# A two-layer encoder trunk on one core: layer 0's u and v projections as three float32r passes instead of one exact float32 pass

## The chip, the cores and the metric

The kernel runs on one core of a Trainium2 chip. The metric is the device time of one execution in microseconds. Times inside the profile count from the start of the profiled span.

## The reference

Two layers, 256 tokens, width 2048. Each layer modulates a layer-normed input by a vector computed from `c`, projects it once into the columns of four head groups, mixes, projects back, and runs a gated convolutional FFN. Cut to what matters here:

```python
for l in range(DEPTH):
    mod = (silu(c) @ w_mod[l] + b_mod[l]).reshape(bn, 6, d)
    shift_m, scale_m, gate_m = mod[:, 0, None], mod[:, 1, None], mod[:, 2, None]
    ...
    h = layer_norm(x) * (1.0 + scale_m) + shift_m
    proj = h @ w_in[l]                       # 2048 -> 4288 columns
    uv, q_c, kv_c, k_r, sb, sc, sh, ag = jnp.split(proj, IN_SPLITS, axis=-1)
    y_a = gmlp_mixer(uv, ...)                # u * (W_s LN(gelu(v)) + b), 512 columns each
    y_b, y_c, y_d = mla_mixer(...), short_conv_mixer(sb, sc, sh, ...), conformer_conv(ag, ...)
    y = jnp.concatenate([y_a, y_b, y_c, y_d], axis=-1) @ w_out[l]
    x = layer_norm(ALPHA * x + (1.0 + gate_m) * y, ...)
    ...                                      # FFN, residual, layer norm
```

## The kernel before

A matmul has two forms. The exact one takes float32 operands. The other takes float32r operands: a tile is split into `hi` (a cast on ScalarE) and `lo` (the difference, on VectorE), and the product is three matmuls, hi·hi, hi·lo and lo·hi. Nearly all of the kernel uses the second form; layer 0's input projection and a few other pieces use the first.

Layer 0's input projection starts in `by_blocks`. The contraction dimension of 2048 is cut into 16 blocks `kt` of 128. The modulation is not known yet, so its shift and scale for one block are computed just ahead of it, and all products that can be started with that block follow:

- two 1 MB tiles `wmod` are loaded and reduced on VectorE (L193, one instruction of 128x2048 each); a small add (`mod`, L1485) finishes the block's two columns, and ScalarE applies them in place to the normed, transposed input (`hF<-hF,mod`, L120, 128x256). `hF` of a block is ready after that;
- D: 1024 columns, 8 products of 128x256 into `accD`; U: 512 columns, 4 of 128x256 into `accU`; V: 512 columns with tokens as rows, 2 of 128x512 into `accV`. Their weights are two tiles `wexact` of 512 KB;
- after each batch of four blocks come E's products for the four (512 columns, two more tiles). `accV` and `accE` share two PSUM buffers, so each is copied away by ScalarE (`partV`, `partE`) at the end of its batch, and the copies of the batches are added on VectorE (L1324).

After `by_blocks` come the latent group B, group C, the attention steps and the output projection; then the FFN and layer 1. In the trace one exact product is two MATMUL records.

The order on each engine is set at build time by a scheduler that places instructions by readiness and program order; at run time each engine takes them in that order. All loads stand on SP's queue. Buffers: 4 for `wmod`, 4 of each of two tags for weight tiles (`wexact` takes the tags in turn), 11 tiles of 4 KB a partition in the pool `slot`, of which `hF` holds four, and 10 in the pool `act`. A load waits on the queue until its buffer is released.

Of the kernel before, what the change touches and what calls it, by code (L numbers as in the profile page):

```python
# [7 lines left out]
F32 = mybir.dt.float32  # L8
F32R = mybir.dt.float32r
AF = mybir.ActivationFunctionType  # L10
ALU = mybir.AluOpType
AX = mybir.AxisListType

P = 128
D = 2048
S = 256
DEPTH = 2
W_G = 512
KT = D // P
# [6 lines left out]
C_UV, C_Q, C_SB, C_SC, C_AG = 0, 1024, 1728, 2240, 3264  # L26
# [21 lines left out]

BATCHES = ((0, 4), (4, 4), (8, 4), (12, 4))

FEED_US, BLOCK_US, LEAD_US = 2.7, 0.432, 6.0

UQ_ORDER = [h * 192 + c for h in range(4) for c in range(128)] + [h * 192 + 128 + c for h in range(4) for c in range(64)]

# [26 lines left out]
def rows_of(l, k0, nk, c0, width):  # L81

    return lambda a: a[l, k0 * P : (k0 + nk) * P, c0 : c0 + width].reshape(nk, P, width).transpose(1, 0, 2)
# [3 lines left out]
def encoder_kernel(ctx: ExitStack, tc: tile.TileContext, A: dict, consts: bass.AP, out: bass.AP):  # L87
    nc = tc.nc
    pe, act, dve, pool = nc.tensor, nc.scalar, nc.vector, nc.gpsimd
# [3 lines left out]
    splitp = ctx.enter_context(tc.tile_pool(name="splitp", bufs=4))  # L93
# [16 lines left out]
    def ms_tile(name):  # L110
        return msp.tile([P, 512], F32, tag="ms", name=name)

    def acc_tile(name):
        return accp.tile([P, 512], F32, tag="acc", name=name)

    def mm(o, lhsT, rhs, start, stop):
        pe.matmul(o, lhsT, rhs, start=start, stop=stop, skip_group_check=True)  # L117
# [4 lines left out]
    def slot(name, dtype=F32):  # L122
        return slotp.tile([P, 1024], dtype, tag="slot", name=name)
# [41 lines left out]
    at = [16 + l * 425 for l in range(DEPTH)]  # L165
# [10 lines left out]
    def rest_of_constants():  # L176
        nc.sync.dma_start(out=par[:, 112:PARAMS], in_=A["params"][:, 112:PARAMS])
        nc.sync.dma_start(out=cst[:, 128:1024], in_=consts[:, 128:1024])
        plus_one(0, SCALE_F, GATE_M, GATE_F)
        plus_one(1, SCALE_M, SCALE_F, GATE_M, GATE_F)  # L180
# [131 lines left out]
    exact_turn = [0]  # L312
# [38 lines left out]
    def act_pair(name):  # L351

        both = actp.tile([P, 4 * S], F32R, tag="act", name=name).rearrange("p (k h t) -> p k h t", k=2, h=2)
        return [both[:, :, 0, :], both[:, :, 1, :], both]
# [6 lines left out]
    def split(dst, src):  # L361
        hi, lo = dst[:2]
        act.copy(hi, src)  # L363
        dve.tensor_tensor(out=lo, in0=src, in1=hi.bitcast(F32), op=ALU.subtract)  # L364
# [907 lines left out]
    def by_blocks(l, w_in, hF, first_mod, quarter, mix_d, mix_u, gelu_v, mix_v, mix_b, mix_c, mix_e):  # L1272


        hf = lambda kt: hF[kt // 4][:, kt % 4, :]
        accD = [acc_tile(f"D{l}_c{i}") for i in range(4)]
        accU = [acc_tile(f"U{l}_c{i}") for i in range(2)]
        parts = {"V": [], "E": []}

        blocks = [lambda kt=kt, m=m: first_mod(kt, m) for kt in range(KT) for m in (SHIFT_M, SCALE_M)]  # L1280
        at = {"mods": 0, "dma": 10.0, "dve": 15.0, "pe": 0.0}
        ready = {}

        def mods_for(kt):

            while at["mods"] < len(blocks) and (
                at["mods"] < 2 * (kt + 1) or at["pe"] - at["dma"] > LEAD_US
            ):
                modulated = blocks[at["mods"]]()
                at["dma"] += FEED_US  # L1290
                at["dve"] = max(at["dve"], at["dma"] + 1.6) + 2.4
                ready[at["mods"] // 2] = at["dve"] + 1.0
                at["mods"] += 1
                if at["mods"] in (2, 4, 6):
                    quarter(at["mods"] // 2, modulated)
                if at["mods"] == 8:
                    rest_of_constants()

        def load(kt, nk, c0, width):

            mods_for(kt + nk - 1)
            got = weights(w_in, kt, nk, c0, width, True)
            at["dma"] += FEED_US * nk * width / 2048
            at["pe"] = max(at["pe"], at["dma"] + 1.6, ready[kt + nk - 1]) + nk * width / P * BLOCK_US
            return [w for w, _ in got]

        def channels(ps, kt, w, start, stop):
            for i in range(w.shape[1] // P):
                o = ps[i // 2][:, (i % 2) * S : (i % 2 + 1) * S]
                mm(o, w[:, i * P : (i + 1) * P], hf(kt), start and i % 2 == 0, stop)  # L1310

        def keep_part(g, ps):
            if len(parts[g]) < len(BATCHES) - 1:
                both = actp.tile([P, 1024], F32, tag="act", name=f"part{g}")
                for i in range(2):
                    act.copy(both[:, i * 512 : (i + 1) * 512], ps[i])
                parts[g].append(both)
            else:
                parts[g].append(ps)

        def total(g):
            *sums, ps = parts[g]
            for other in sums[1:]:
                dve.tensor_tensor(out=sums[0], in0=sums[0], in1=other, op=ALU.add)  # L1324
            halves = [sums[0][:, i * 512 : (i + 1) * 512] for i in range(2)]
            for i in range(2):
                dve.tensor_tensor(out=halves[i], in0=ps[i], in1=halves[i], op=ALU.add)
            return halves

        quarter(0, None)  # L1330
        mods_for(0)
        for k0, nkt in BATCHES:
            accV = [ms_tile(f"V{l}_{t}") for t in range(2)]
            for kt in range(k0, k0 + nkt):
                d, uv = load(kt, 1, C_AG, 1024)[0], load(kt, 1, C_UV, 1024)[0]

                def product_v(kt=kt, uv=uv):
                    for t in range(2):
                        mm(accV[t], hf(kt)[:, t * P : (t + 1) * P], uv[:, 512:], kt == k0, kt == k0 + nkt - 1)

                def product_du(kt=kt, d=d, uv=uv):
                    channels(accD, kt, d, kt == 0, kt == KT - 1)
                    channels(accU, kt, uv[:, :512], kt == 0, kt == KT - 1)

                for product in (product_v, product_du) if kt == k0 + nkt - 1 else (product_du, product_v):
                    product()
            keep_part("V", accV)
            if k0 + nkt == KT:
                mix_d(accD, None)
                mix_u(accU, None)  # L1350
                for t, v in enumerate(total("V")):
                    gelu_v(t, v)
            es = []
            for kt in range(k0, k0 + nkt, 2):
                es.extend(load(kt, 2, C_SB, 512))
            accE = [ms_tile(f"E{l}_{i}") for i in range(2)]
            for kt, w in enumerate(es, k0):
                channels(accE, kt, w, kt == k0, kt == k0 + nkt - 1)
            keep_part("E", accE)
        sumE = total("E")  # L1360
        postponed.append(mix_v)
        phase(l, "B")
        run(latent_group(w_in, C_Q, f"B{l}", mix_b, hF=hf, bg=STEPS[l]["B"]))
        phase(l, "C")

        def mix_ce(cps, tps):
            mix_c(cps, tps)
            mix_e(sumE, None)

        run(group(w_in, C_SC, 1024, f"C{l}", mix_ce, hF=hf, bg=STEPS[l]["C"]), 2)  # L1370
# [154 lines left out]
    for l in range(DEPTH):  # L1525
        Y = {}
        if l == 0:
            hF = [slot(f"hF{q}").rearrange("p (j s) -> p j s", j=4) for q in range(4)]
            quarter, powers = normed_T(hF)
            mixers(l, (A["w_in"], l), Y, hF, first_mod_of(hF, powers), quarter)  # L1530
        else:
            mixers(l, (A["w_in"], l), Y)
        phase(l, "out")
        out_proj(
            l,
            "out",
            (A["w_out"], l),
            lambda i, Y=Y: Y["abcd"[i]],
            list(range(KT)),
            gate(l, GATE_M),  # L1540
            f"o{l}",
            A["post_mix_g"][l],
            A["post_mix_b"][l],
            needs(l, SHIFT_F, SCALE_F),
            modulated(l, SHIFT_F, SCALE_F),
            plain=(1024, 1536) if l == 0 else (),
            bg=STEPS[l]["out"],
        )
        phase(l, "up")
        G = []  # L1550
        ffn_up(l, G)
        phase(l, "down")
        out_proj(
            l,
            "down",
            (A["ffn_w_down"], l),
            lambda i, G=G: G[i],
            list(range(NF)),
            gate(l, GATE_F),
            f"d{l}",  # L1560
            A["post_ffn_g"][l],
            A["post_ffn_b"][l],
            needs(l + 1, SHIFT_M, SCALE_M) if l + 1 < DEPTH else None,
            modulated(l + 1, SHIFT_M, SCALE_M) if l + 1 < DEPTH else None,
        )
# [88 lines left out]
```

## Time and profile before

| | us |
|---|---|
| median of 3 runs | 2214.95 (2213.76 to 2219.54) |
| profiled execution | 2214.94 |
| its span | 2213.2 |
| `by_blocks` on TensorE: first product to the first of B | 21.03 to 161.73 |
| one block of D, U and V inside a batch | 6.90 |
| one batch (E end to E end) | 34.49 |

The profiled execution is the median run to 0.01 us; 1.74 us lie outside its span. Over the whole span TensorE (PE) is busy 99%, VectorE (DVE) 77%, ScalarE (ACT) 49%. Busy of PE is modelled from the records of matmuls and hides gaps of a fraction of a microsecond, so the pace of PE is read from the starts of its rows. A row of the timeline gives start, duration, engine, line, operation, output and inputs, shape and count, and in brackets the idle time just before it and what ended it.

### The profile page before, as it was taken

The numbers are of one execution on the slowest core, as the hardware profiler recorded it, in microseconds if no ns is written. First come the engines' busy times: TensorE is split into PE (matmuls) and PEld (weight loads), VectorE is DVE, ScalarE is ACT, GpSimd is POOL, SyncE is SP. The second block draws the span as 40 slices with busy tenths as digits, with TensorE's granted clock in tenths as the row PEclk, the third lists the DMA queues.
The fourth block names the chain that finished last, engine by engine and source line by source line (L and its number), as shares of the span: only waits on it lengthen the run. The fifth ranks groups of instructions, "written<-read, shape, count | busy, mean of one in ns | idle before, by whom it ended". The sixth has DMA issues, their size and how long they took to land. (4 is left out here: it accounts for less than half of the span.)

```text
span 2213.2 us, 28318 instructions
## 1 busy us (share of the span) xinstructions
PE 2185.3 (99%) x10852; PEld 1794.0 (81%) x10852; DVE 1702.1 (77%) x2265; ACT 1075.7 (49%) x1652; POOL 22.4 (1%) x38
## 2 busy tenths in 40 slices
PE   9999999999999999999999999999999999999997
PEld 6776875588888888888867988868888888888886
DVE  5657996799898888989958988877765656565776
ACT  3132730655454545545665455465444545464553
POOL 0000000000000000000000000000000000000000
PEclk9999999999999999999999999999999999999999
DMA  9999889598888888888757547856765555555553
GB/s 391 417 376 391 358 332 390 210 350 324 310 333 318 327 313 324 344 332 326 285 215 294 189 157 255 316 210 246 265 211 190 190 190 191 190 210 192 191 195 145
DMA packets 94730, 608.15 MB, mean 275 GB/s; under 512 B 10689, under 2 KB 10881, under 8 KB 29313
## 3 DMA queue, kind: packets, MB, share of 16 engines
q1 hardware_dynamic: 94466, 606.31, 74.0%
q8 instruction: 85, 1.39, 0.2%
q14 instruction: 51, 0.42, 0.0%
q10 hardware_dynamic: 128, 0.03, 0.0%
HBM read 604.17 MB, written 2.13 MB: 274 GB/s over the span
## 5 line engine op out<-in xcount | busy, mean ns | idle before, releaser
L345 DVE TENSOR_TENSOR wlo<-wraw,whi 128x1024 fp32r<-128x1024 f32 (+1 forms) x608 | 729.0, 1214 | 286.3 <-ACT whi L344 273.1
L344 ACT CAST whi<-wraw 128x1024 fp32r<-128x1024 f32 (+1 forms) x608 | 630.9, 1045 | 635.4 <-PE g_c L117 207.8
L193 DVE SCALAR_TENSOR_TENSOR wmod<-wmod,crep 128x2048 f32<-128x2048 f32 x192 | 438.4, 2287 | 72.0 <-DMA wmod<-in_w_mod_dram 71.1
L117 PE MATMUL v_c<-hT,whi 128*128 128x512 f32 x1408 | 489.7, 393 | 0.0
L117 PE MATMUL g_c<-hT,whi 128*128 128x512 f32 x1280 | 445.0, 392 | 0.0
L117 PE MATMUL v_c<-hT,wlo 128*128 128x256 f32 x1408 | 392.5, 279 | 0.0
L117 PE MATMUL d<-whi,a 128*128 128x512 f32 x1344 | 386.5, 389 | 0.0
L117 PE MATMUL g_c<-hT,wlo 128*128 128x256 f32 x1280 | 356.8, 279 | 0.4 <-DVE wlo L345 0.4
L117 PEld LDWEIGHTS v_c<-hT,whi 128*128 128x128 f32 x1408 | 263.6, 187 | 59.2
L117 PEld LDWEIGHTS d<-whi,a 128*128 128x128 f32 x1344 | 252.0, 188 | 52.4
L117 PEld LDWEIGHTS g_c<-hT,whi 128*128 128x128 f32 x1280 | 239.7, 187 | 54.1
L117 PEld LDWEIGHTS v_c<-hT,wlo 128*128 128x128 f32 x1408 | 265.4, 188 | 0.2
L117 PEld LDWEIGHTS g_c<-hT,wlo 128*128 128x128 f32 x1280 | 241.2, 188 | 0.7 <-DVE wlo L345 0.7
L117 PE MATMUL d<-wlo,a 128*128 128x512 f32 x672 | 232.9, 389 | 0.0
L117 PEld LDWEIGHTS d<-wlo,a 128*128 128x128 f32 x672 | 126.1, 188 | 26.2
L363 ACT CAST a<-g 128x512 fp32r<-128x512 f32 x132 | 81.3, 617 | 63.8 <-PE d L117 63.2
L364 DVE TENSOR_TENSOR a<-g,a 128x512 fp32r<-128x512 f32 x132 | 89.0, 686 | 5.1 <-ACT a L363 5.1
L117 PE MATMUL o<-whi,a 128*128 128x512 f32 x320 | 91.6, 393 | 0.0
L501 PE MATMUL first<-wexact,hN 128*128 128x512 f32 x192 | 85.5, 595 | 1.4 <-ACT hN L120 1.0
L1415 DVE SCALAR_TENSOR_TENSOR u<-g,par,u 128x254 f32<-128x254 f32 (+1 forms) x176 | 73.8, 477 | 0.0
L117 PEld LDWEIGHTS o<-whi,a 128*128 128x128 f32 x320 | 60.6, 190 | 12.7
L501 PEld LDWEIGHTS first<-wexact,hN 128*128 128x128 f32 x192 | 35.3, 190 | 41.2 <-issue 34.9
(311 smaller groups left out, 2174.0 us busy)
## 6 DMA issues: line engine op xcount, KB each, us to landing
wmod<-in_w_mod_dram SPq DMA_DIRECT2D x192, 1024.0 KB, 7.2
wraw<-in_ffn_w_up_dram SPq DMA_DIRECT2D x168, 1024.0 KB, 5.1
wraw<-in_ffn_w_down_dram SPq DMA_DIRECT2D x88, 1024.0 KB, 5.0
wexact<-in_w_in_dram SPq DMA_DIRECT2D x64, 512.0 KB, 11.0
wraw<-in_w_in_dram SPq DMA_DIRECT2D x24, 1024.0 KB, 6.1
wraw<-in_w_out_dram SPq DMA_DIRECT2D x22, 1024.0 KB, 6.0
wexact<-in_w_out_dram SPq DMA_DIRECT2D x20, 512.0 KB, 11.6
wexact<-in_ffn_w_up_dram SPq DMA_DIRECT2D x16, 512.0 KB, 5.7
```

The lines of the kernel that those rows point to most:

```text
L117: pe.matmul(o, lhsT, rhs, start=start, stop=stop, skip_group_check=True)
L193: i = dve.scalar_tensor_tensor(out=raw, in0=raw, scalar=1.0, in1=crep, op0=ALU.mult, op1=ALU.mult, accum_out=col)
L344: held(act.copy(hi[:, :m], r), "cast")
L345: i = dve.tensor_tensor(out=lo[:, :m], in0=r, in1=hi[:, :m].bitcast(F32), op=ALU.subtract)
L363: act.copy(hi, src)
L364: dve.tensor_tensor(out=lo, in0=src, in1=hi.bitcast(F32), op=ALU.subtract)
L501: i = pe.matmul(ps, hN[kt // 4][:, kt % 4, t * P : (t + 1) * P], parts[kt], start=kt == 0, stop=kt == KT - 1, skip_group_check=True,)
L1415: dve.scalar_tensor_tensor(out=u[:, sh:], in0=x[:, : S - sh], scalar=col(k, j), in1=u[:, sh:], op0=ALU.mult, op1=ALU.add)
```

## The change

For every block, the 1024 columns of u and v are loaded into one tile `wuv` (same size and buffers as before) and split: ScalarE casts 128x1024 into `hi_uv`, VectorE subtracts into `lo_uv`, both in tiles of the pool `slot`. The block's `hF` is split too: ScalarE casts 128x256 into the first half of `h`, VectorE subtracts into the second. V becomes 6 products of 128x512 and U 12 of 128x256 in float32r. D and E stay exact. Each block's loads now stand as two `wmod`, D's tile, `wuv`; before, one `wexact` stood between the two `wmod` at most blocks. Three tiny memsets on GpSimd touch `hF`'s later tiles at the start, so that they hold their slots.

```diff
+        def load_split(kt):
+            at["dma"] += FEED_US / 2
+            at["pe"] = max(at["pe"], at["dma"] + 3.0, ready[kt]) + 8 * SPLIT_US
...
+            raw = splitp.tile([P, 1024], F32, tag=tag, name="wuv")
...
+            hi, lo = slot("hi_uv", F32R), slot("lo_uv", F32R)
+            act.copy(hi, raw)
+            dve.tensor_tensor(out=lo, in0=raw, in1=hi.bitcast(F32), op=ALU.subtract)
+            if kt % 2 == 0:
+                halves["h"] = act_pair("h")
+            h = [x[:, kt % 2, :] for x in halves["h"][:2]]
+            split(h, hf(kt))
+            return hi, lo, h
...
-                d, uv = load(kt, 1, C_AG, 1024)[0], load(kt, 1, C_UV, 1024)[0]
...
+                d = load(kt, 1, C_AG, 1024)[0]
+                hi, lo, (xh, xl) = load_split(kt)
+                st, sp = kt == k0, kt == k0 + nkt - 1
+                if not sp:
+                    channels(accD, kt, d, kt == 0, False)
+                for t in range(2):
+                    tok = slice(t * P, (t + 1) * P)
+                    mm(accV[t], xh[:, tok], hi[:, 512:], st, False)
+                    mm(accV[t], xh[:, tok], lo[:, 512:], False, False)
+                    mm(accV[t], xl[:, tok], hi[:, 512:], False, sp)
+                if sp:
+                    channels(accD, kt, d, False, kt == KT - 1)
+                st, sp = kt == 0, kt == KT - 1
+                for i in range(4):
...
+                    mm(o, hi[:, off], xh, st and i % 2 == 0, False)
+                    mm(o, hi[:, off], xl, False, False)
+                    mm(o, lo[:, off], xh, False, sp)
...
+            for q in range(1, 4):
+                pool.memset(hF[q][:, 0, 0:1], 0.0)
```

The new instructions take places in the order of VectorE and ScalarE. VectorE from the second half of block 9 to the modulation of block 10 (`sums_9` is block 9's pair of `wmod`, the x2 is both of block 10's, `partE` the addition of the batches' E). Before:

```order
L193 SCALAR_TENSOR_TENSOR wmod,sums_9_544<-wmod,crep 128x2048
L1324 TENSOR_TENSOR partE<-partE 128x1024
L193 SCALAR_TENSOR_TENSOR wmod,sums_9_544<-wmod,crep 128x2048
L1485 TENSOR_TENSOR mod_9_553<-sums_9_544,par 128x2
L193 SCALAR_TENSOR_TENSOR wmod,sums_10_572<-wmod,crep 128x2048 x2
L1485 TENSOR_TENSOR mod_10_581<-sums_10_572,par 128x2
```

VectorE in the same stretch after the change:

```order
L193 SCALAR_TENSOR_TENSOR wmod,sums_9_695<-wmod,crep 128x2048
L364 TENSOR_TENSOR h<-hF_120,h 128x256
L1344 TENSOR_TENSOR partE<-partE 128x1024
L1320 TENSOR_TENSOR lo_uv<-wuv,hi_uv 128x1024
L193 SCALAR_TENSOR_TENSOR wmod,sums_9_695<-wmod,crep 128x2048
L1512 TENSOR_TENSOR mod_9_739<-sums_9_695,par 128x2
L364 TENSOR_TENSOR h<-hF_120,h 128x256
L1320 TENSOR_TENSOR lo_uv<-wuv,hi_uv 128x1024
L193 SCALAR_TENSOR_TENSOR wmod,sums_10_778<-wmod,crep 128x2048 x2
L1512 TENSOR_TENSOR mod_10_785<-sums_10_778,par 128x2
```

Both subtractions of block 9 now stand ahead of block 10's two reductions, and those of block 8 ahead of the second reduction of block 9. ScalarE in the same stretch, from block 8's modulation to block 10's, before:

```order
L120 ACTIVATE hF_120<-hF_120,mod_8_514 128x256
L1316 COPY partE<-E_0_521 128x512
L1316 COPY partE<-E_1_522 128x512
L120 ACTIVATE hF_120<-hF_120,mod_9_553 128x256
L120 ACTIVATE hF_120<-hF_120,mod_10_581 128x256
```

ScalarE there after the change:

```order
L120 ACTIVATE hF_120<-hF_120,mod_8_667 128x256
L1336 COPY partE<-E_0_672 128x512
L363 CAST h<-hF_120 128x256
L1336 COPY partE<-E_1_673 128x512
L1319 CAST hi_uv<-wuv 128x1024
L120 ACTIVATE hF_120<-hF_120,mod_9_739 128x256
L363 CAST h<-hF_120 128x256
L1319 CAST hi_uv<-wuv 128x1024
L120 ACTIVATE hF_120<-hF_120,mod_10_785 128x256
```

Each block's cast of the weights stands behind that block's own modulation and its cast of `hF`. In the first batch the order is a little different; VectorE there from block 0's sum to block 2's reductions, before:

```order
L1485 TENSOR_TENSOR mod_0_198<-sums_0_191,par 128x2
L193 SCALAR_TENSOR_TENSOR wmod,sums_1_221<-wmod,crep 128x2048 x2
L1485 TENSOR_TENSOR mod_1_244<-sums_1_221,par 128x2
L193 SCALAR_TENSOR_TENSOR wmod,sums_2_265<-wmod,crep 128x2048 x2
```

VectorE in that stretch after the change:

```order
L1512 TENSOR_TENSOR mod_0_201<-sums_0_194,par 128x2
L1320 TENSOR_TENSOR lo_uv<-wuv,hi_uv 128x1024
L193 SCALAR_TENSOR_TENSOR wmod,sums_1_259<-wmod,crep 128x2048
L364 TENSOR_TENSOR h<-hF_118,h 128x256
L193 SCALAR_TENSOR_TENSOR wmod,sums_1_259<-wmod,crep 128x2048
L1512 TENSOR_TENSOR mod_1_266<-sums_1_259,par 128x2
L1320 TENSOR_TENSOR lo_uv<-wuv,hi_uv 128x1024
L364 TENSOR_TENSOR h<-hF_118,h 128x256
L193 SCALAR_TENSOR_TENSOR wmod,sums_2_321<-wmod,crep 128x2048 x2
```

Here too each block's subtractions stand ahead of the next block's reductions; on ScalarE two normalising `xn` stand between a block's modulation and its cast of the weights in blocks 0 to 2. Behind `by_blocks` the four compute engines' order is that of before but for a few neighbours that change places on VectorE in group B.

More of the change, by code (lines that the diff above doesn't have):

```diff
@@ L49 @@
 BATCHES = ((0, 4), (4, 4), (8, 4), (12, 4))
-FEED_US, BLOCK_US, LEAD_US = 2.7, 0.432, 6.0
+FEED_US, BLOCK_US, SPLIT_US, LEAD_US = 2.7, 0.432, 0.35, 6.0
 UQ_ORDER = [h * 192 + c for h in range(4) for c in range(128)] + [h * 192 + 128 + c for h in range(4) for c in range(64)]
@@ L1305, in load @@
             return [w for w, _ in got]
+        halves = {}
+        def load_split(kt):
+            at["dma"] += FEED_US / 2
+            at["pe"] = max(at["pe"], at["dma"] + 3.0, ready[kt]) + 8 * SPLIT_US
+            tag = ("whi", "wlo")[exact_turn[0] % 2]
+            exact_turn[0] += 1
+            raw = splitp.tile([P, 1024], F32, tag=tag, name="wuv")
+            w, l = w_in
+            nc.sync.dma_start(out=raw, in_=w.take(1024, rows_of(l, kt, 1, C_UV, 1024)))
+            hi, lo = slot("hi_uv", F32R), slot("lo_uv", F32R)
[6 more added lines that the diff above has]
+            return hi, lo, h
         def channels(ps, kt, w, start, stop):
@@ L1334, in by_blocks @@
             for kt in range(k0, k0 + nkt):
-                d, uv = load(kt, 1, C_AG, 1024)[0], load(kt, 1, C_UV, 1024)[0]
[L1337 to L1346, printed above, removed]
+                d = load(kt, 1, C_AG, 1024)[0]
[12 more added lines that the diff above has]
+                for i in range(4):
+                    o = accU[i // 2][:, (i % 2) * S : (i % 2 + 1) * S]
+                    off = slice(i * P, (i + 1) * P)
+                    mm(o, hi[:, off], xh, st and i % 2 == 0, False)
+                    mm(o, hi[:, off], xl, False, False)
+                    mm(o, lo[:, off], xh, False, sp)
             keep_part("V", accV)
```

## The prediction

> **What bounds the kernel now.** I read the page's first lines for the whole, then the stretches of the changed stage, then each engine's timeline there.
>
> ```profile
> PE 2185.3 (99%) x10852; PEld 1794.0 (81%) x10852; DVE 1702.1 (77%) x2265; ACT 1075.7 (49%) x1652; POOL 22.4 (1%) x38
> 92.75:127.24 34.49, 34.49 (x145) 27.36 (x144) 21.04 (x22) 4.74 (x8) 0.00 (x0) 1.00 1.02 417
> 162.00:201.00 39.00, 39.00 (x143) 25.69 (x142) 33.64 (x36) 9.58 (x27) 0.00 (x0) 1.00 0.93 367
> ```
>
> The first row says that TensorE (PE) never rests for long, so what lengthens or shortens its chain shows in the end. The second is the third batch of `by_blocks` (after the time: PE, weight loads, VectorE, ScalarE, GpSimd, granted clock, DMA share, GB/s): PE full, VectorE busy 21 of 34 us, ScalarE 5, the DMA engines full at 417 GB/s. The third is group B, full on PE. Inside the batch PE goes from block to block without a stop:
>
> ```profile
> 92.75 3.62 PE L117 MATMUL D_c<-hF,wexact 128*128 128x256 f32 x16
> 96.20 1.89 PE L117 MATMUL U_c<-hF,wexact 128*128 128x256 f32 x8
> 97.93 1.88 PE L117 MATMUL V<-wexact,hF 128*128 128x512 f32 x4
> 99.64 3.62 PE L117 MATMUL D_c<-hF,wexact 128*128 128x256 f32 x16
> 120.33 7.07 PE L117 MATMUL E<-hF,wexact 128*128 128x256 f32 x32
> 127.24 3.62 PE L117 MATMUL D_c<-hF,wexact 128*128 128x256 f32 x16
> 161.73 0.81 PE L117 MATMUL B_w<-wexact,hF 128*128 128x384 f32 x2
> ```
>
> From start to start D takes 3.45 us, U 1.73, V 1.71, a block 6.9, E 6.91. The stage ends at 161.73, where B starts.
>
> **The change: PE's own work.** A float32r product's pace stands in layer 1:
>
> ```profile
> 1205.68 2.08 PE L117 MATMUL Da_c<-hT,wlo 128*128 128x256 f32 x16
> 1207.59 3.82 PE L117 MATMUL Da_c<-hT,whi 128*128 128x512 f32 x16
> 1211.25 2.08 PE L117 MATMUL Da_c<-hT,wlo 128*128 128x256 f32 x16
> ```
>
> 16 of 128x256 take 1.91 us, 0.119 each; 16 of 128x512 take 3.66, 0.229 each. So V becomes 6 x 0.229 = 1.37 us, U 12 x 0.119 = 1.43. A block goes from 6.9 to 6.25 us, and 16 blocks save 16 x 0.64 = 10.2 us of PE work. That is the whole gain, if PE remains the one that ends last.
>
> **What must be ready for a block.** The added conversions are small beside the idle time of their engines, but they stand in strict order with what makes the next block's input:
>
> ```profile
> 131.61 2.28 DVE L193 SCALAR_TENSOR_TENSOR wmod<-wmod,crep 128x2048 f32<-128x2048 f32 x1
> 133.82 2.28 DVE L193 SCALAR_TENSOR_TENSOR wmod<-wmod,crep 128x2048 f32<-128x2048 f32 x1
> 136.15 0.16 DVE L1485 TENSOR_TENSOR mod<-sums,par 128x2 f32<-128x2 f32 x1
> 136.34 0.60 ACT L120 ACTIVATE hF<-hF,mod 128x256 f32<-128x256 f32 x1 [4.02 <-DVE mod L1485]
> L344 ACT CAST whi<-wraw 128x1024 fp32r<-128x1024 f32 x592 | 618.3, 1052 | 615.0 <-PE g_c L117 207.8 <-PE v_c L117 153.2 <-PE d L117 136.0
> L345 DVE TENSOR_TENSOR wlo<-wraw,whi 128x1024 fp32r<-128x1024 f32 x592 | 714.7, 1222 | 286.3 <-ACT whi L344 273.1 <-issue 5.5 <-PE Da_c L117 2.0
> L363 ACT CAST hT<-hN 128x512 fp32r<-128x512 f32 x24 | 14.5, 617 | 0.0
> 153.30 0.60 ACT L785 ACTIVATE sg<-D_c 128x512 f32<-128x512 f32 x1 [0.27 <-PE D_c L117]
> 153.93 0.69 DVE L786 TENSOR_TENSOR gluD<-D_c,sg 128x512 f32<-128x512 f32 x1 [0.17 <-ACT sg L785]
> ```
>
> Reductions follow each other by 2.21 us, the sum comes 2.33 after the second, `hF` starts 0.19 later and takes 0.60. Casts of 512 and 1024 columns take 0.617 and 1.052, so one of 256 about 0.40. The subtraction of 1024 takes 1.22, and I let the next instruction start 1.15 after it. ScalarE hands to VectorE in 0.03 (153.30 + 0.60 to 153.93).
>
> After the change VectorE may start block k+1's reductions only behind block k's `lo_uv`, which waits for block k's cast of the weights, which on ScalarE stands behind block k's `hF` and its cast. The loop from `hF` to the next `hF` is therefore 0.60 + 0.03 (cast of `hF` starts) + 0.40 + 1.05 + 0.03 + 1.15 + 2.21 + 2.33 + 0.19 = 7.99 us. The small subtraction (about 0.4) lies beside the cast of the weights. Against 6.25 on PE, PE now waits about 1.7 us ahead of each such block, and its saving is gone inside the batch.
>
> **Batches 2 to 4.** Does E's time let VectorE run ahead? No: the cast of the next batch's first block stands behind the first copy of E, and its weights' cast behind the second.
>
> ```profile
> 92.08 0.59 ACT L1316 COPY partE<-E 128x512 f32<-128x512 f32 x1 [2.82 <-PE E L117]
> 92.95 0.59 ACT L1316 COPY partE<-E 128x512 f32<-128x512 f32 x1 [0.28 <-PE E L117]
> 93.56 1.23 DVE L1324 TENSOR_TENSOR partE<-partE 128x1024 f32<-128x1024 f32 x1 [2.79 <-ACT partE L1316]
> ```
>
> E ends at 92.75 here. The second copy ends 0.79 after, the weights' cast 1.05 later; VectorE adds `partE` from +0.81 and starts `lo_uv` at about +1.97, the second reduction of block 9 at +3.1, its sum at +5.45, `hF` is done at +6.25. PE needs it at 3.45 + 2.8 = 6.25: no wait. Blocks 10 and 11 then start at +14.3 and +22.3. In the batch's last block V waits for `lo_uv` in the middle of D, about 0.1, and the block and E take 6.25 + 0.1 + 6.9. The batch is 35.6 us instead of 34.5: three of them cost 3 x 1.1 = +3.3. Loads allow this: a batch brings 13.6 MB (8 x 1024 KB and 10 x 512 KB), at 417 GB/s 32.7 us. The smallest this term could be is the DMA's pace, 32.7, where three batches gain 5.4; the largest comes with 0.3 us more a hand-over in the two loops, +1.2 a batch.
>
> **The first batch.** Its rows in the profile:
>
> ```profile
> 18.65 0.60 ACT L120 ACTIVATE hF<-hF,mod 128x256 f32<-128x256 f32 x1
> 19.15 1.50 ACT L120 ACTIVATE xn<-x,rs_in 128x512 f32<-128x512 f32 x2
> 18.32 2.29 DVE L193 SCALAR_TENSOR_TENSOR wmod<-wmod,crep 128x2048 f32<-128x2048 f32 x1
> 42.60 3.19 PE L117 MATMUL D_c<-hF,wexact 128*128 128x256 f32 x14
> 51.35 1.03 PE L117 MATMUL E<-hF,wexact 128*128 128x256 f32 x4
> ```
>
> Block 1's first reduction, at 18.32 before, stands behind `lo_uv` of block 0: both `xn` end at 20.65, cast to 21.7, subtraction, so 22.9. Then reduction, the small subtraction (0.34), reduction, sum: `hF` of block 1 is done at 28.55. In these blocks the two `xn` (1.4) and the small subtraction (0.34) lie in the loop, and the cast of `hF` does not: 7.99 - 0.40 + 1.40 + 0.34 = 9.3. Block 2 is ready at 37.9, block 3 (two more small instructions, 0.25) at 47.5. PE would have asked at 34.8 and at 44.2: it waits 3.1 and 3.3 us. D of block 3 starts at 47.5 instead of 42.60, +4.9. From there to E it was 51.35 - 42.60 = 8.75 us with transposes among it; now 0.64 less, plus about 0.4 for V's waits. E of the first batch starts at 56.0, +4.7. Bounds: nothing, if PE never waited (even -2.6 by its own work), and +6 with 0.3 us on each of four hand-overs.
>
> **What waits cost beside themselves.**
>
> ```profile
> 212.00:216.00 4.00, 1.66 (x6) 0.79 (x6) 4.00 (x9) 1.16 (x4) 0.00 (x0) 1.00 1.00 401
> 216.00:220.00 4.00, 3.99 (x11) 3.28 (x12) 3.27 (x3) 2.43 (x7) 0.00 (x0) 0.57 1.03 409
> 213.11 0.67 PE L117 MATMUL ps_kr<-kc,cst 64*128 64x256 f32 x2 [1.25 <-DVE kc L1053]
> 216.01 2.50 PE L117 MATMUL ps_qn<-qg,wq 128*128 128x256 f32 x5 [1.24 <-DVE kvr L1057]
> ```
>
> After 4 us with PE busy 1.66, in two waits of about 1.25, the granted clock was 0.57 over the next 4 us: 0.43 x 4 = 1.7 us of work lost. Inside a batch such a loss hides in the next wait; ahead of a batch's last block it lengthens the batch. Ahead of block 3 PE waits 3.3 us, so that about half of the surrounding 6 us is idle; ahead of blocks 7, 11 and 15 it waits 1.7 us in 8, PE busy nearly 80%. I take half of one loss, 0.9, between 0 and 4 x 1.7 = 6.8. The Trainium skill ("TensorE: Matmul & The Clock Gate", HAM oscillation) holds that the clock falls only where PE idles for more than some 3.4 us; by that rule no wait here would cost anything and the sum would be 0.9 lower. The rows above are against it, since the clock fell with no wait over 1.25 us.
>
> **The sum.** +4.7 + 3.3 + 0.9 = +8.9 us at the end of `by_blocks` (170.6 instead of 161.7). Behind it the order of every engine is the same as before but for a few neighbours on VectorE, B is full on PE, and its loads wait for buffers that VectorE and PE release, so they move with the stage; I carry the 8.9 to the end. The profiled execution has 2214.94 (span 2213.2 and 1.74 around it), and the runs' median is 2214.95: 2223.8, rounded to 2224. The memsets on GpSimd (0.1 each) end before anything waits for that engine.
>
> **The rivals.**
>
> *The conversions run beside PE and the 10.2 us are won.* That is the other side: 2214.9 - 10.2 = 2204.7, or about 2206 if the DMA's 32.7 a batch (0.8 us over PE's 31.9) decides. For it speak the busy shares, VectorE 21 of 34.5 us. It decides where the loop falls under PE's new block of 6.25; it pays nothing above 6.9. With the weights' cast and its subtraction's wait off the loop it would be 6.9. The order on ScalarE puts that cast behind `hF`, so I give it 7%.
>
> *The shift is taken back later.* Behind B PE stops of its own:
>
> ```profile
> 201.00:216.00 15.00, 10.99 (x51) 7.82 (x49) 10.60 (x13) 6.14 (x21) 1.63 (x3) 1.00 1.01 417
> ```
>
> PE rests 4.0 of 15 us there, with the DMA full. If loads that were early by then fill this hole, 4.0 come back and the time is 2220, no measurable change. Against it: SP's loads in B stand behind released buffers. The same result comes if the hand-overs and waits are a little cheaper than I add them. 23%.
>
> *The clock falls at every batch.* Then +4.7 + 3.3 + 6.8 = 14.8: 2229.7. The row of 0.57 speaks for it, PE's 80% ahead of blocks 7, 11 and 15 against. 15%.
>
> *Float32r passes cost no less than exact ones here* would change little, since PE is not last inside the batch: 0.64 for each batch's last block, under +3. It is in the range.
>
> **Numbers.** The forecast's own case, 2221.6 to 2227, gets 53%, the rivals 7, 23 and 15, and 2% lie beyond. The measurement can tell 0.3%, 6.6 us: slower means over 2221.6. Slower 0.53 + 0.15 + 0.01 = 0.69, same 0.23 + 0.01 = 0.24, faster 0.07. The range from 2217 to 2230 leaves out the gain, the far side of the second rival and the far side of the third, below 2 in 10.
>
> **What would show it.** B's first product near 170.6; `hF` of neighbouring blocks in a batch 8.0 us apart (9.3 in the first); D's start 1.7 us after V and U have ended, with the wait put to `hF`; VectorE waiting for `hi_uv` and `h`, not for `wmod` loads; U's and V's products 2.8 us a block; a lower DMA rate in the stage; the rest of the kernel as before, shifted. I am wrong if blocks follow each other by under 6.9 us, or if B's start is late and the end is not.

## The result, and the profile after

| | before | after |
|---|---|---|
| median of 10 runs, us | 2214.12 (2213.19 to 2219.54) | 2220.86 (2218.75 to 2226.28) |
| ratio of the runs | | 1.0030 (95%: 1.0022 to 1.0038) |
| first product of B on TensorE, us | 161.73 | 168.53 |
| profiled execution: time, span | 2214.94, 2213.2 | 2224.31, 2222.5 |

The change makes the kernel 6.7 us slower; 8.9 were forecast. The profiled execution of after is 3.45 us over its median: from about 650 us on, far behind the change, a pair of products (128x512 and 128x256) takes 0.353 us, where before takes 0.347 until about 850; that is 1.9% more, at a granted clock of 1.00 in both, and the cause is not known. Up to there all positions can be compared, and nothing below rests on that stretch.

The page's first line and the third-batch window of after (the columns as in the prediction's window):

```profile
PE 2183.7 (98%) x10948; PEld 1801.5 (81%) x10948; DVE 1726.8 (78%) x2297; ACT 1097.3 (49%) x1684; POOL 22.5 (1%) x41
92.75:127.24 34.49, 31.80 (x166) 27.80 (x165) 26.35 (x29) 9.93 (x16) 0.00 (x0) 1.00 0.98 386
```

In the stretch where PE was full it now rests 2.69 of 34.49 us, VectorE has 5.3 us more work and still idles 8.1, ScalarE has 5.2 more, and the loads fell from 417 to 386 GB/s. No compute engine is full, and no reduction waits for its load (the waits under experiment 1): a chain is the limit. TensorE's timeline of after shows where it rests (the brackets):

```profile
55.70 7.07 PE L117 MATMUL E<-hF,wexact 128*128 128x256 f32 x32
97.79 3.62 PE L117 MATMUL D_c<-hF,wexact 128*128 128x256 f32 x16
104.06 3.72 PE L117 MATMUL D_c<-hF,wexact 128*128 128x256 f32 x16
111.96 3.72 PE L117 MATMUL D_c<-hF,wexact 128*128 128x256 f32 x16 [1.35 <-ACT hF L120]
119.85 1.99 PE L117 MATMUL D_c<-hF,wexact 128*128 128x256 f32 x8 [1.34 <-ACT hF L120]
133.16 3.62 PE L117 MATMUL D_c<-hF,wexact 128*128 128x256 f32 x16
168.53 0.81 PE L117 MATMUL B_w<-wexact,hF 128*128 128x384 f32 x2
```

Without a wait a block takes 104.06 - 97.79 = 6.27 us; the next two follow after 7.90 and 7.89, each behind a wait of some 1.35 for `hF`. The batch takes 133.16 - 97.79 = 35.37. ScalarE and VectorE in one turn of the loop, from block 9's `hF` to block 10's, in after:

```profile
103.41 0.60 ACT L120 ACTIVATE hF<-hF,mod 128x256 f32<-128x256 f32 x1 [3.89 <-DVE mod L1512]
104.04 0.41 ACT L363 CAST h<-hF 128x256 fp32r<-128x256 f32 x1
104.35 1.04 ACT L1319 CAST hi_uv<-wuv 128x1024 fp32r<-128x1024 f32 x1
105.43 1.23 DVE L1320 TENSOR_TENSOR lo_uv<-wuv,hi_uv 128x1024 fp32r<-128x1024 f32 x1 [0.52 <-ACT hi_uv L1319]
106.57 2.28 DVE L193 SCALAR_TENSOR_TENSOR wmod<-wmod,crep 128x2048 f32<-128x2048 f32 x1
108.78 2.29 DVE L193 SCALAR_TENSOR_TENSOR wmod<-wmod,crep 128x2048 f32<-128x2048 f32 x1
111.11 0.16 DVE L1512 TENSOR_TENSOR mod<-sums,par 128x2 f32<-128x2 f32 x1
111.30 0.60 ACT L120 ACTIVATE hF<-hF,mod 128x256 f32<-128x256 f32 x1 [5.91 <-DVE mod L1512]
```

111.30 - 103.41 = 7.89 us, where 7.99 were summed. Each row starts where the one before lets it. VectorE waits for `hi_uv`.

### The profile page after: what moved, and what is told of

The parts are those of the page before. It is cut to its first block, busy times and chain, and to the rows that moved or that the text cites. A ratio compares the mean times of both kernels' runs of the same rounds, so it can differ in the third digit from the quotient of the medians.

```text
span 2222.5 us, 28589 instructions
## 1 busy us (share of the span) xinstructions
PE 2183.7 (98%) x10948; PEld 1801.5 (81%) x10948; DVE 1726.8 (78%) x2297; ACT 1097.3 (49%) x1684; POOL 22.5 (1%) x41
## 5 line engine op out<-in xcount | busy, mean ns | idle before, releaser
L193 DVE SCALAR_TENSOR_TENSOR wmod<-wmod,crep 128x2048 f32<-128x2048 f32 x192 | 437.4, 2284 | 35.6 <-DMA wmod<-in_w_mod_dram 34.6
L117 PE MATMUL D_c<-hF,wexact 128*128 128x256 f32 x256 | 62.7, 391 | 12.2 <-ACT hF L120 12.2
```

The source lines that it names most:

```text
L193: i = dve.scalar_tensor_tensor(out=raw, in0=raw, scalar=1.0, in1=crep, op0=ALU.mult, op1=ALU.mult, accum_out=col)
```

## The experiments

The changed kernel puts two things into one edit: PE's cheaper passes, and a conversion whose place on two in-order engines closes a loop. The theory is that the place costs all that is lost, namely the loop above, in which each block's reductions stand behind the conversion of the block before. Its rivals: the amount of converting costs, the passes themselves cost, or the loads are the limit. Ratios are to the kernel before, on the same chip.

### 1. Weights' cast ahead of the modulation, `lo_uv` behind the block's own sum

```diff
+                cast = load_cast(kt)          # load wuv, act.copy(hi, raw)
                 d = load(kt, 1, C_AG, 1024)[0]
-                hi, lo, (xh, xl) = load_split(kt)
+                hi, lo, (xh, xl) = split_rest(kt, *cast)
 ...
-            dve.tensor_tensor(out=lo, in0=raw, in1=hi.bitcast(F32), op=ALU.subtract)
+            i = dve.tensor_tensor(out=lo, in0=raw, in1=hi.bitcast(F32), op=ALU.subtract)
+            tc.add_manual_dep(i.ins, summed[kt], order_dep, reason="the block's own sum comes first")
```

The load of `wuv` moves ahead of D's tile with the cast; experiment 2 has that too.

> All conversions stay, in the same number and size. In the program the load and the cast of a block's u and v weights stand ahead of the block's modulation, and the subtraction `lo_uv` is ordered behind the block's own sum on VectorE. Own theory (the loop from `hF` to the next `hF` through the cast of the weights is what costs): the weights' cast now runs beside the reductions, the loop falls to about 6.2 us, PE's 6.25 a block or the loads (3.1 MB a block, 7.5 us at 417 GB/s, when nothing is loaded ahead) decide, B starts at 154 to 158 us, time 2206 to 2211 us, ratio to before 0.997 to 0.9985. Rival (the amount of converting on VectorE and ScalarE costs, wherever it stands): B stays at 167 to 170, 2219 to 2222 us. Second rival (the loads bound the stage, as before): B at 161 to 162, about 2214.

Measured: 2207.91 us, ratio 0.9980 (0.9956 to 1.0004; one execution of six took 2225.10 and widens it). Run once more beside another kernel:

> The kernel with the weights' cast first and `lo_uv` behind the sum once more, beside the one with both orders, for a narrower interval: 2207 to 2208.5, ratio to before 0.997 to 0.9977. Rival (its first median of 6 runs was low by chance): 2210 or more.

2207.76, ratio 0.9968 (0.9955 to 0.9981). Its two medians agree, and the second interval is clear of 1. The third batch, VectorE in two of its blocks, the waits between 58 and 150 us (us in total, times, longest), and the start of B, in the first of these runs:

```profile
91.22:123.80 32.58, 32.27 (x169) 28.37 (x168) 27.38 (x30) 10.13 (x17) 0.00 (x0) 1.00 1.02 417
...
102.19 0.16 DVE L1520 TENSOR_TENSOR mod<-sums,par 128x2 f32<-128x2 f32 x1
102.30 1.23 DVE L1324 TENSOR_TENSOR lo_uv<-wuv,hi_uv 128x1024 fp32r<-128x1024 f32 x1
103.47 0.43 DVE L364 TENSOR_TENSOR h<-hF,h 128x256 fp32r<-128x256 f32 x1
104.85 2.29 DVE L193 SCALAR_TENSOR_TENSOR wmod<-wmod,crep 128x2048 f32<-128x2048 f32 x1 [0.96 <-DMA wmod<-in_w_mod_dram]
...
DVE wmod L193 <- DMA wmod<-in_w_mod_dram: 5.8, 14, 1.0
...
DVE lo_uv L1324 <- ACT hi_uv L1318: 2.7, 2, 1.3
...
PE D_c L117 <- ACT hF L120: 0.7, 2, 0.4
...
156.44 0.81 PE L117 MATMUL B_w<-wexact,hF 128*128 128x384 f32 x2
```

`lo_uv` doesn't wait here, and only twice in the whole stretch; the reductions now wait for their loads. The batch (the window's ends are D's first products) is 32.58 us long at 417 GB/s, as the prediction's 13.6 MB at that rate gave (32.7), and the fourth 32.64; the second takes 31.98, which is PE's own work. So the loads are the limit of the last two, by 0.6 to 0.7 us each. The same conversions, in the same number, and 13 us less than in the changed kernel.

Not all of PE's 10.2 us come through: B is 5.3 us earlier than before. Most of what is missing lies in the first batch, whose E starts at 52.33, 1.0 later than before (51.35), though PE's own work ahead of it is 2.6 less.

In the waits of after between 58 and 150 us, loads of `wmod` don't appear; the rows of PE and of `lo_uv` there are

```profile
PE D_c L117 <- ACT hF L120: 6.7, 5, 1.4
DVE lo_uv L1320 <- ACT hi_uv L1319: 5.2, 9, 1.1
```

### 2. The same without the order for `lo_uv`

```diff
-            tc.add_manual_dep(i.ins, summed[kt], order_dep, reason="the block's own sum comes first")
```

> As the first, but without the order for `lo_uv`: on VectorE it then stands between the small subtraction of one block and the reductions of the next, and waits for a cast that stands behind the cast of `hF` on ScalarE. Own theory: the loop is the same eight instructions long as in the changed kernel, 7.9 us, B starts at 167 to 170, time 2219 to 2222. Rival (what matters is only that the weights' cast stands ahead of `hF` on ScalarE): the loop is gone, 2206 to 2211.

Measured: 2222.18, ratio 1.0038 (1.0024 to 1.0053). ScalarE, VectorE, block 3 and E of the first batch with the clock between them, and the start of B:

```profile
106.25 0.60 ACT L120 ACTIVATE hF<-hF,mod 128x256 f32<-128x256 f32 x1 [3.89 <-DVE mod L1517]
107.19 1.04 ACT L1318 CAST hi_uv<-wuv 128x1024 fp32r<-128x1024 f32 x1
108.26 1.23 DVE L1324 TENSOR_TENSOR lo_uv<-wuv,hi_uv 128x1024 fp32r<-128x1024 f32 x1 [0.52 <-ACT hi_uv L1318]
114.14 0.60 ACT L120 ACTIVATE hF<-hF,mod 128x256 f32<-128x256 f32 x1 [5.91 <-DVE mod L1517]
...
48.30 0.50 PE L117 MATMUL V<-hi_uv,h 128*128 128x512 f32 x1 [3.09 <-ACT h L363]
50.00:54.00 4.00, 4.00 (x17) 3.42 (x18) 3.96 (x6) 1.24 (x3) 0.00 (x0) 0.57 1.03 412
58.57 7.07 PE L117 MATMUL E<-hF,wexact 128*128 128x256 f32 x32
171.31 0.81 PE L117 MATMUL B_w<-wexact,hF 128*128 128x384 f32 x2
```

The cast and subtraction here are those of the next block, so by name the cast is early; by place they stand in the loop as before, and it is 114.14 - 106.25 = 7.89 us long. One order on one subtraction a block is worth 14 us. B is 2.8 us later than in the changed kernel, 1.3 more than the upper end expected; that comes from the first batch (E at 58.57 instead of 55.70). Block 3 starts 1.28 us later there (48.30 instead of 47.02), behind a wait of 3.09. Behind this wait the granted clock falls, and from block 3 to E PE takes 10.27 us; in the second run of experiment 1, where no clock falls, the same stretch, also with V first, takes 8.69 (43.18 to 51.87). No later wait takes this loss up, so some 1.6 us of the 14 are the clock's, brought about by the longer wait.

### 3 and 4. Exact products with the conversions kept, in both orders

```diff
-                    mm(accV[t], xh[:, tok], hi[:, 512:], st, False)
-                    mm(accV[t], xh[:, tok], lo[:, 512:], False, False)
-                    mm(accV[t], xl[:, tok], hi[:, 512:], False, sp)
+                    mm(accV[t], hf(kt)[:, tok], raw[:, 512:], st, sp)
 ...                                       # U alike, in the order of before
```

> The conversions stay as in the changed kernel, but u and v are computed in the exact products of before, so PE's block is 6.9 us again. Own theory: PE is not last inside a batch, the blocks stay 7.9 us apart (9.2 in the first batch), and only the last block of each batch gets longer, by 0.6: 2222 to 2225. Rival (the float32r passes themselves, or a lower clock in them, cost the time): about 2214, as before.

> All conversions kept in the better order (weights' cast first, `lo_uv` behind the sum), but u and v in the exact products of before. Own theory: the loop of about 6.2 is under PE's 6.9 a block, so the conversions cost nothing but some start: B at 161.5 to 163, 2213.5 to 2215.5; the 6 us that the same order gains with three passes are then PE's saving, cut off by the loads. Rival (the better order itself gains, with or without three passes): 2207 to 2210. Second rival (conversions cost whatever their place): 2217 or more.

Measured: in the changed kernel's order 2221.68, ratio 1.0037 (1.0023 to 1.0051), 0.3 under the range expected; in the order of experiment 1 2213.41, ratio 0.9996 (0.9987 to 1.0005). TensorE in the first of the two, and B in the second:

```profile
111.88 3.72 PE L117 MATMUL D_c<-hF,wexact 128*128 128x256 f32 x16 [0.21 <-ACT hF L120]
119.78 0.70 PE L117 MATMUL D_c<-hF,wexact 128*128 128x256 f32 x2 [0.73 <-ACT hF L120]
169.65 0.81 PE L117 MATMUL B_w<-wexact,hF 128*128 128x384 f32 x2
```

```profile
162.09 0.81 PE L117 MATMUL B_w<-wexact,hF 128*128 128x384 f32 x2
```

With 0.63 us more work a block PE waits less, but blocks follow 119.78 - 111.88 = 7.90 us apart as before. The kernels so far make a table (medians, us):

| | exact u, v | three passes |
|---|---|---|
| no conversions | 2214.1 | |
| conversions in the loop | 2221.7 | 2220.9 |
| conversions out of the loop | 2213.4 | 2207.8 |

Inside the loop the passes bring 0.8, outside it 5.6 (by B's first product 1.1 and 5.7). With exact products the conversions cost 7.6 inside it and nothing outside.

### 5. Weights converted once

```diff
+            if kt == 0:
+                halves["w"] = ...            # hi_uv, lo_uv of block 0
+            hi, lo = halves["w"]
```

> The three passes and the split of `hF` stay; of the weights only block 0's are converted and used for all 16 blocks (the others are loaded and not used), so the result is not the reference's. Own theory: without the weights' cast and subtraction the loop is 0.60 + 0.03 + 0.40 + 0.03 + 0.36 + 2.21 + 2.33 + 0.19 = 6.15 us; PE or the loads decide: 2205 to 2211, near the first kernel of this set. If it is over 2 us below that one, the work of converting costs beside its place. Rival (PE's passes bring no gain because the loads bound the stage): 2213 to 2215.

Measured: 2207.83, ratio 0.9967 (0.9955 to 0.9979), the time of experiment 1. Fifteen casts of 1.05 us and fifteen subtractions of 1.23 are gone, and nothing more is gained: the amount of converting costs nothing that the time shows where the loop is open. B does start at 155.55, 0.9 before that of experiment 1, but the C products behind the next waits start at 217.65 and 217.56: between 208 and 215 us the clock is at 0.51 here, a longer fall than in experiment 1.

### 6. First batch exact

```diff
+                if k0 == 0:
+                    ...                      # loads and products of before
+                    continue
```

> The changed kernel, but batch 1 (blocks 0 to 3) keeps the exact products and has no conversions. Own theory (the loop costs 0.7, 0.9 and 0.9 us in batches 2 to 4 and 4.3 in the first, and the two add up): the first batch as before, B starts at 164.2 us, time 2216 to 2217.5 us. Rival (all of it is lost in the first batch, and the later ones only follow it late): B at 161.7, 2214. Second rival (an early first batch lets later batches lose more, since only there the loop decides): B at 166 or later, over 2218.

Measured: 2213.29, ratio 1.0004 (0.9995 to 1.0013). My own numbers missed, and those of the first rival were nearly met (B at 161.61), but not for its reason: the first batch was as before and batches 3 and 4 took 35.37 us each, so the loss isn't all in the first batch; the second took 32.85. VectorE in it, where the reduction at 62.80 belongs to block 6 and the subtraction to block 5:

```profile
62.80 2.28 DVE L193 SCALAR_TENSOR_TENSOR wmod<-wmod,crep 128x2048 f32<-128x2048 f32 x1
65.35 1.22 DVE L1320 TENSOR_TENSOR lo_uv<-wuv,hi_uv 128x1024 fp32r<-128x1024 f32 x1
66.48 2.29 DVE L193 SCALAR_TENSOR_TENSOR wmod<-wmod,crep 128x2048 f32<-128x2048 f32 x1
161.61 0.81 PE L117 MATMUL B_w<-wexact,hF 128*128 128x384 f32 x2
```

The scheduler, with a different start, put one reduction ahead of `lo_uv`, and that turn of the loop is one reduction (2.2 us) shorter; PE's waits in the batch fall from 2.63 to 0.57. So the run doesn't tell the two terms apart as meant; it shows that one neighbour in the order is worth 2.3 us in a batch.

### 7. `xn` behind the casts in the first batch

```diff
-                    quarter(at["mods"] // 2, modulated)
+                    late.append(...)         # called behind the cast of h, ordered behind it
```

> The changed kernel, but in blocks 0 to 2 the two `xn` stand behind the casts of `h` and of the weights on ScalarE, and not ahead of them. Own theory: the loop of the first batch falls from 9.2 to 7.9 us, block 3 can start at 43.2 instead of 47.0, E of the first batch at 51.9 instead of 55.7, the later batches as they were: B at 164.7, time 2216.5 to 2218. Rival (the loads, 7.5 us a block, hold the first batch anyway): some 0 to 1 us of gain, 2220 to 2221.

Measured: 2216.19, ratio 1.0014 (1.0006 to 1.0023). TensorE:

```profile
42.75 1.56 PE L117 MATMUL D_c<-hF,wexact 128*128 128x256 f32 x6 [1.40 <-ACT hF L120]
51.57 7.07 PE L117 MATMUL E<-hF,wexact 128*128 128x256 f32 x32
164.41 0.81 PE L117 MATMUL B_w<-wexact,hF 128*128 128x384 f32 x2
```

E starts 4.13 us earlier than in the changed kernel and B 4.12, each 0.3 more than expected: two small instructions in the loop of three blocks were nearly the whole first term, and what is gained there stays to the end (4.7 in the medians). The later batches take 35.2 and 35.4 as before.

### 8. Fewer loads in the kernel of experiment 1

```diff
+                if kt % 2 == 0:
                     d = load(kt, 1, C_AG, 1024)[0]
```

> The kernel with the cast of the weights first and `lo_uv` behind the sum (2207.9 us), but D's weight tile is loaded for every other block alone and used twice, so the result is not the reference's: 8 x 0.52 = 4.2 MB less, 10 us at 417 GB/s. Own theory (the loads are what now holds that kernel at 32.6 us a batch): batches fall to PE's 31.9, VectorE no longer waits for `wmod` loads, B starts at 152 to 155 instead of 156.4, time 2203 to 2206. Rival (the loop of conversions still holds it): B at 156, 2207 to 2209.

Measured: 2205.81, ratio 0.9966 (0.9954 to 0.9978), B at 155.20. The third batch's stretch:

```profile
92.70:127.20 34.50, 33.59 (x176) 29.64 (x176) 28.29 (x33) 10.02 (x16) 0.00 (x0) 1.00 0.96 379
96.19 3.72 PE L117 MATMUL D_c<-hF,wexact 128*128 128x256 f32 x16 [0.91 <-ACT hF L120]
```

The DMA engines are no longer full, and no reduction waits for a load between 58 and 150 us, so those waits were the loads'. Of the 10 us of loads that are gone the time fell by 2.1: the first batch is 2.4 us shorter (E at 49.94 instead of 52.33), so the loads held that batch too; the second takes 31.99, as in experiment 1, but batches 3 and 4 take 33.18, half a microsecond more than with all loads, with a new wait of 0.91 for their second block. In this kernel's order both reductions of that block stand behind the addition of `partE` on VectorE, in experiment 1 one of them ahead of it. So the time expected (2203 to 2206) was met at its upper end, B missed its range by 0.2, and batches 3 and 4 of 31.9 were not seen: what these two would take with this order unchanged and fewer loads stays open.

### 9. Spare products in PE's first long wait

```diff
+                if kt == 1:
+                    for _ in range(20):
+                        mm(accU[0][:, :P], ident, zeros, False, False)
```

> The changed kernel with 20 spare products of 128x128 with zeros (0.12 us each) on PE between blocks 1 and 2, where it waits 2.63 us and its clock then falls to 0.77 and 0.80. Own theory: the granted clock stays at 1.00, D of block 2 takes 3.45 us instead of 5.05, but PE then waits that much longer for `hF` of block 3: B at 168.5 and 2220 to 2222 as without. Rival (the lower clock is part of the loss): B 1.0 to 1.6 us earlier, 2219 to 2220. Second rival (the clock falls anyway, for another reason than PE's wait): D of block 2 again 5.05 us.

Measured: 2219.56, ratio 1.0026 (1.0014 to 1.0038), an interval that overlaps that of the changed kernel. The time lies in the rival's range (2219 to 2220) and not in mine, so the rows have to decide. The same four microseconds and the wait ahead of them, first in after, then here:

```profile
37.80 5.41 PE L117 MATMUL D_c<-hF,wexact 128*128 128x256 f32 x16 [2.63 <-ACT hF L120]
38.00:42.00 4.00, 4.00 (x12) 3.21 (x12) 1.88 (x3) 2.40 (x4) 0.00 (x0) 0.57 1.04 420
47.02 1.56 PE L117 MATMUL D_c<-hF,wexact 128*128 128x256 f32 x6 [1.00 <-ACT hF L120]
```

```profile
38.00:42.00 4.00, 4.00 (x25) 3.67 (x24) 2.33 (x3) 1.94 (x3) 0.00 (x0) 1.00 1.04 419
46.57 2.86 PE L117 MATMUL D_c<-hF,wexact 128*128 128x256 f32 x12 [1.12 <-ACT hF L120]
168.00 0.81 PE L117 MATMUL B_w<-wexact,hF 128*128 128x384 f32 x2
```

The clock stayed up. (An exact product is two records, so the spare ones took 4.5 us and held block 2 up by over a microsecond, which I had not counted.) Block 3 still started when its `hF` came. B is 0.53 earlier, but this execution's first product was 0.65 earlier too (20.10 against 20.75). In the changed kernel the fallen clock had cost nothing.

### 10. Both orders together

The edits of experiments 1 and 7 in one kernel.

> The weights' cast first, `lo_uv` behind the block's sum, and in blocks 0 to 2 the two `xn` behind the cast of `h`: both changes of order together. Own theory: the loads already hold the stage without the second change (B at 156.4), so it brings little: B at 155 to 156.4, 2206.5 to 2208. Rival (the gains of the two orders add, 6.0 below before and 4.7 below the changed kernel): B near 152.3, 2203 to 2204.

Measured: 2207.39, ratio 0.9961 (0.9949 to 0.9974), B at 156.34: as expected, the gains don't add where the loads are the limit. It is not told apart from experiment 1, and both beat the kernel before by 6 to 7 us and the changed kernel by 13.

## Why the prediction was right, and where it was not

- **PE's own work**: forecast 6.25 us a block, measured 6.27. Right; the rival that float32r brings no saving is out.
- **The loop**: 7.99 summed, 7.89 measured; in the first batch 9.3 and 9.2. That this loop is the cause, and not the amount of converting, is shown by experiments 1 and 2, which differ in one order, and by 3 to 5.
- **Batches 2 to 4**: forecast 35.6 each, +3.3 in all; measured 35.18 (from E's end), 35.37 and 35.37, +2.45. A term a third too large: the loop's 0.1 counts twice in a batch, and in batch 2 no `partE` is added, which I had in all three.
- **The first batch**: forecast +4.7 at E's start, measured 55.70 - 51.35 = +4.35. Nearly right, with another inside: PE waited 2.63 and 1.00 us ahead of blocks 2 and 3 and not 3.1 and 3.3. Of the 2.3 that are missing ahead of block 3, 1.6 are the clock's, which fell between them, so that D of block 2 took 5.05 us instead of 3.45. Experiment 7 shows that the two `xn` are the cause.
- **The clock**: forecast +0.9, paid 0. This step failed in its place: I looked for the fall ahead of block 3, where it would have lengthened the stage. It came after the wait for block 2 and lay ahead of the next wait, which took it up (experiment 9). In experiment 2 it came ahead of block 3 as well and was paid, some 1.6 us, near the 1.7 of the forecast's one loss: the price was right, the place was not. Ahead of blocks 7, 11 and 15 it did not fall. The rival of a fall at every batch is out.
- **The sum**: +8.9 forecast for B's start, +6.80 measured (4.35 + 2.45): 0.9 of the miss is the clock, 0.85 the later batches, 0.35 the first.
- **Carried to the end**: right. B's shift of 6.80 is 6.62 behind the place where PE rests (C's products at 229.58 instead of 222.96), and the medians differ by 6.74. The rival of a shift taken back there is out. Its time, 2220, lay near the measured one because my terms were too large together, which the prediction had named as the other way to the same result ("hand-overs and waits are a little cheaper than I add them").
- **The rival on the other side** had the right point of decision: with the cast and the subtraction's wait off the loop the loads decide, 2206 forecast, 2207.8 measured in experiment 1. Its sum was short: 0.8 us a batch over 2204.7 gives 2207.1 with three batches, and the 2.6 us that PE saves in the first batch didn't come through in experiment 1.

2220.86 lies in the range of 2217 to 2230, but just under the 2221.6 to 2227 of my own case. By its words "slower means over 2221.6" the result is not slower, though the interval of the ratio, 1.0022 to 1.0038, is clear of 1. The loop and the path to the end were right; the sum is 2.1 us too large since all three of its terms were.

The start of the C products behind the place where PE rests, before and after:

```profile
222.96 11.39 PE L117 MATMUL C_c<-hF,wexact 128*128 128x256 f32 x52
229.58 11.39 PE L117 MATMUL C_c<-hF,wexact 128*128 128x256 f32 x52
```

## What to carry to other kernels

When work is added to engines with idle time, don't ask how long it is but which turn of a recurrence it stands in: write down, per engine, the order of one turn and sum the hand-overs, then compare with the engine that is full. Where two in-order engines feed each other, move an added piece to the side on which its input is ready early and its result is needed late; here one order on one subtraction was worth 14 us. Look next at what becomes the limit: here some 6 of the 10 us that PE saves come through, and the loads hold part of the first batch and the last two.

## What the runs showed of the hardware that I had not expected

TensorE's granted clock fell behind waits of about 2 us and more, and not always behind the same ones. In this stage it fell behind waits of 1.97, 2.16, 2.28, 2.63 and 3.09 us (experiments 3, 1 and 2, after, and experiment 2 again), to 0.59 over 4 us in the first and 0.57 in the last two. D behind the first four took 5.05 to 5.24 us instead of 3.45. It did not fall behind 1.75 (experiment 10), nor behind shorter single waits. In group C, two waits of 1.22 and 1.24 within some 4 us did it in one execution of the kernel of experiment 1, and 0.33 and 1.24 did not in the other. The 8 us around that place, in the first run and in the second:

```profile
208.00:216.00 8.00, 6.76 (x23) 5.00 (x23) 5.95 (x7) 4.42 (x11) 0.00 (x0) 0.79 1.02 412
```

```profile
208.00:216.00 8.00, 6.76 (x32) 5.62 (x31) 6.97 (x8) 7.07 (x18) 0.00 (x0) 1.00 1.03 414
```

Their spans are 2205.8 and 2202.4, and the executions of this kernel and of experiment 10 fall into two groups, near 2204.4 and near 2207.7 (but for one of 2225.1 and one of 7823.4). The profile of experiment 10, with a span of 2202.8, has waits of 0.34 and 1.24 there and no fall. That the clock makes the groups is argued from these three profiles alone. The Trainium skill ("TensorE: Matmul & The Clock Gate", HAM oscillation) sets the bound at gaps of more than some 3.4 us, which these rows contradict. The Trainium skill ("TensorE: Matmul & The Clock Gate", What's actually happening) has the cold clock at half rate, and full again after at least one busy window of some 3.4 us. An estimate from this 3.4 us of the Trainium skill is (4 - 0.5 x 3.4) / 4 = 0.575 over 4 us, near the 0.57 and 0.59 here; in group C of experiment 2 the fall lasted about 7 us (0.52 from 224 to 231 us), some two such windows.
